# Strassen's scheme for the values of a chunked recurrence, inside a fused HGRN2 + MLA layer

## The chip, the cores and the metric

The kernel is one launch on one core of a Trainium2 chip. The metric is device time of that launch in microseconds (us), the median of a few runs, before against after. A difference under about 0.2% (1.2 us) can't be told from no change here.

## The reference, cut to what matters

One hybrid decoder layer over 512 tokens of 1024 channels. Its first product projects the normalised input onto many column groups; two branches follow, a gated linear recurrence (HGRN2, 8 heads of 128) and multi-head latent attention (MLA), merged by gates:

```
h  = rms_norm(x, g)                              # (512, 1024)
hq, hf, hi, hz, cq, ckv, kr, mz, glog = split(h @ w_in)
v  = hi                                          # the recurrence's values: h @ w_in[:, 2048:3072]
S_t = diag(f_t) S_{t-1} + k_t v_t^T ;  o_t = S_t^T q_t        # chunkwise, per head
y_a = rms_norm(o) * silu(hz) ;  y_b = MLA(cq, ckv, kr) * silu(mz)
m  = sigmoid(g_a) * (y_a @ W_pa) + sigmoid(g_b) * (y_b @ W_pb)
out = rms_norm(x + m @ W_out)
```

The change is about `v`: a 512x1024 by 1024x1024 product. All is float32; each product runs as three matmuls of a high and a low part (hi*hi, hi*lo, lo*hi), so each weight tile is first cast to its high part (ScalarE, line 129) and the rest subtracted (VectorE, line 130).

## The kernel before, in words

**Stages in order of time.** (1) `x` is loaded, normalised, transposed into `hT` (two parts), and the latent columns `c` are projected, in an order written out by hand. (2) The second part of `c` is projected, then `c` is transposed into `cT`. (3) Four head pairs of the recurrence, `hg_pair(0)` to `hg_pair(3)`: each projects F (forget), Q and ZA (gate) with `proj_ch`, and pairs 0 and 2 also project the values of four heads with `proj_tok` (line 606). `hg_forget` makes decays on VectorE and GpSimd, `hg_turned`, `hg_states`, `hg_scores`, `hg_out` and `hg_gate` are small matmuls and elementwise work. (4) Eight MLA heads. (5) The two merge gates, `W_pa`, `W_pb` and `W_out`. The gates, `W_pa` and `W_out` already use a Strassen scheme with seven products (`strassen`, line 943).

**Values before.** `proj_tok` takes 512 columns and runs over four token tiles, eight k-slices and three kinds: 96 matmuls of 512 columns, in pair 0 and again in pair 2. Each reads four weight chunks of 512 KB.

**Order of the work.** Outside blocks marked manual, a planner orders each engine's queue from a simulated timeline; `issue_after` only forbids an earlier place. Each engine works through its own queue in order.

**Weights.** `load_w` takes one of three raw buffers (SP's queue), one of four high and one of four low buffers. After each load it issues one entry of `queued`: copies of weight blocks from HBM to HBM for `BlockSums`, which `step()` later adds to by accumulating transfers on GpSimd's queue (line 803).

**Sums of the activations.** `early_sums(q)` (line 819) makes the four differences of blocks of `hT` that the gates' Strassen products need, half in `hg_pair(0)` behind its forget part, half behind pair 0, and saves them to HBM.

**Memory.** The `cwork` pool (`c_sb`, `ktab` and others) is closed before `mla_a` and `hgrn` are opened; `ya` is a plain tile, first written by `hg_gate`.

Of the kernel before, what the change touches and what calls it, by code (L numbers as in the profile page):

```python
# [18 lines left out]
P = 128  # L19
# [4 lines left out]
H = 8  # L24
# [14 lines left out]
def hybrid_layer(ctx: ExitStack, tc: tile.TileContext, a):  # L39
# [68 lines left out]
    queued = []  # L108

    def load_w(*pieces, to=None):  # L110
# [4 lines left out]
        for src in pieces:  # L115
# [12 lines left out]
            o += n  # L128
        last_hi[0] = nc.scalar.copy(hi[:, :o], raw[:, :o])  # L129
# [51 lines left out]
    kpe = Pair(cpool.tile([P, 2, S], F32R, "kpe")[:])  # L181
    cw = Pool("cwork", "right")
# [23 lines left out]
    x_sb = [st.tile([P, D], F32, "x", bufs=NT) for _ in range(NT)]  # L206
# [49 lines left out]
    def squares(t):  # L256
        sq = st.tile([P, D], F32, "sq", bufs=2)
        nc.scalar.activation(sq[:], x_sb[t][:], AF.Square, accum_out=rss[t][:, 0:1])
        power(rss[t][:, 0:1], rss[t][:, 0:1], 1.0 / D, EPS, neg_half[:, 0:1])
# [17 lines left out]
    def c_product(t, kh, kind, ks=range(4)):  # L277
# [3 lines left out]
        for k in ks:  # L281
            nc.tensor.matmul(ps, hT[l][:, 4 * kh + k, t * P : t * P + P], c_hl[kh][r][:, k * 256 : k * 256 + 256],  # L282
                             start=kh == 0 and kind == 0 and k == 0, stop=kh == 1 and kind == FIN and k == 3)

# [7 lines left out]
    with tc.manual_schedule(engines={mybir.EngineType.PE, mybir.EngineType.Activation, mybir.EngineType.DVE}):  # L292
# [49 lines left out]
        for t in range(1, NT):  # L342
            if t + 2 < NT:
                squares(t + 2)
            for kh in range(2):
                lo[kh]()
# [47 lines left out]
    c_second += [load_c2(j) for j in range(2, 4)]  # L394
    for t in range(NT):
# [4 lines left out]
        nc.scalar.copy(c_sb[:, t, 256:704], ps[:, 0:448])  # L400
    css = cw.tile([P, 2, NT], F32, "css")
# [6 lines left out]
    kd = cw.tile([P, NT, 2, NR], F32, "kd")  # L408
# [17 lines left out]
    ps = ax_tile()  # L426
    for t in range(NT):
        nc.tensor.transpose(ps[:, t * P : t * P + P], kd[:, t].rearrange("p a r -> p (a r)"), ident[:])
    split(*kpe, ps[:])
# [3 lines left out]
    ya = ypool.tile([P, H, S], F32, tag="ya", name="ya")  # L433
    ma_pool = Pool("mla_a", "right")
    qtab = ma_pool.tile([P, 2, S], F32, "qtab")
    nc.gpsimd.dma_start(qtab[:], a["c_qtab"])
# [120 lines left out]
    def hg_out(h, asb, st_, q128, v_sb):  # L557
# [12 lines left out]
        nc.vector.tensor_tensor(on[:].rearrange("p (g v) -> p g v", g=NT), ops[:].rearrange("p (g v) -> p g v", g=NT),  # L570
# [15 lines left out]
    v_sb = [None] * NT  # L586

    def hg_pair(pair, in_forget=None, in_query=None, before_gate=None, last=None):
        cc, hs = pair * 256, (2 * pair, 2 * pair + 1)
        pf = proj_ch(w_in, COL_F + cc, hT)  # L590
# [3 lines left out]
        else:  # L594
            early_sums(kh[0])
# [7 lines left out]
        if pair % 2 == 0:  # L603
            for t in range(NT):
                v_sb[t] = hw.tile([P, 512], F32, f"v{t}")
            proj_tok(w_in, COL_I + cc, hT, lambda t, ps: nc.scalar.copy(v_sb[t][:], ps[:]))
        else:
            zz = gate()
        pq = proj_ch(w_in, COL_Q + cc, hT)
        qq = [hg_query(h, pq[i], kk[i][0], kk[i][2], None if i else in_query) for i, h in enumerate(hs)]  # L610
        step()
# [4 lines left out]
        if pair % 2 == 0:  # L616
# [27 lines left out]
    def mla_turn(pair):  # L644
# [4 lines left out]
        for b in range(4):  # L649
            nc.scalar.dma_start(qs[32 * b : 32 * b + 32, :], qr[32 * (b ^ 1) : 32 * (b ^ 1) + 32, :])  # L650
# [122 lines left out]
    kh = [slice(0, 2), slice(2, 4)]  # L773
    half_t = [slice(0, 256), slice(256, 512)]
    blocks = lambda t: (t[:, 0:4, half_t[0]], t[:, 4:8, half_t[0]], t[:, 0:4, half_t[1]], t[:, 4:8, half_t[1]])
    TERMS = ((0, 0), (1, 1), (0, 1), (1, 0))

    def minus(out, x, y):
        nc.vector.tensor_tensor(out, x, y, op=ALU.subtract)

    def minus_minus(out, x, y):

        nc.vector.scalar_tensor_tensor(out, x, -1.0, y, op0=ALU.mult, op1=ALU.subtract)

    class BlockSums:
# [7 lines left out]
        def start(self):  # L793
            for t, ij in zip(self.t, TERMS):
                for q in kh:
                    queued.append(lambda t=t[:, q], w=self.w[ij][:, q]: nc.sync.dma_start(t, w))

        def add(self, *ns):
            with tc.issue_after(last_pool[0].ins):
                for n in ns:  # L800
                    x = {0: self.w[0, 1], 2: self.w[1, 1], 1: self.t[0], 3: self.t[1]}[n]
                    for q in kh:
                        nc.gpsimd.dma_start(self.t[n][:, q], x[:, q], accum_op=ALU.add)
# [13 lines left out]
    h_dram = [[dram.tile([P, 4, 256], F32, name=f"h{n}{i}") for i in range(2)] for n in range(1, 5)]  # L817
# [496 lines left out]
```

## Time and profile before

| | us |
|---|---|
| median of 3 runs | 607.22 (606.46 to 607.28) |
| the profiled execution, its own time | 606.81 |
| its span, first to last instruction | 605.0 |
| outside the span | 1.8 |

The profile is one execution. PE is TensorE's matmul queue, PEld its weight loads, DVE VectorE, ACT ScalarE, POOL GpSimd, SP the queue that issues most transfers. "Busy" of PE includes the modelled end of each matmul, so two matmuls overlap in it; the distance between starts is what one costs in a stream.

### The profile page before, as it was taken

The page shows a single profiled execution, that of the slowest core. Times are in us where ns is not written, and L with a number is a line of the kernel's source. Part 1 is how long each engine was busy: PE and PEld are TensorE (multiplying, and loading weights), DVE is VectorE, ACT ScalarE, POOL GpSimd, SP SyncE. Part 2 cuts the span into 40 slices and gives each one's busy share as a digit, 9 for nine tenths or more (in the row PEclk, how much of TensorE's full clock was granted, in tenths as well). Part 3 has the DMA queues.
Part 4 walks back from the last instruction along what each step waited for, and adds up shares of the span by engine and source line. Part 5 has one row for each costly group of instructions (what it writes and reads, how often), then busy time and mean ns, then how long its engine had stood idle before and what let it go on. Part 6 is the DMA issues. An engine that isn't in the chain of part 4 may idle for free.

```text
span 605.0 us, 8841 instructions
## 1 busy us (share of the span) xinstructions
PE 595.2 (98%) x3198; PEld 501.4 (83%) x3198; DVE 430.1 (71%) x697; ACT 282.1 (47%) x517; POOL 159.5 (26%) x256
## 2 busy tenths in 40 slices
PE   8999999999999999999999999999999999999994
PEld 5998888888888888888888888888888888888884
DVE  6717988477654648768767686778878878466795
ACT  6555154333314332436555554456656764253553
POOL 3107602384460238524245440300000000000003
PEclk9999999999999999999999999999999999999998
DMA  8449579989889866772369676787666655467313
GB/s 274 157 141 334 171 251 381 261 168 278 209 175 273 174 198 119 186 148 65 68 156 169 153 157 158 203 301 244 190 193 202 196 186 187 134 225 262 105 36 139
DMA packets 73035, 115.34 MB, mean 191 GB/s; under 512 B 7560, under 2 KB 37662, under 8 KB 72992
## 3 DMA queue, kind: packets, MB, share of 16 engines
q1 hardware_dynamic: 63740, 90.99, 46.4%
q0 software_dynamic: 8336, 22.55, 20.8%
q10 hardware_dynamic: 916, 1.25, 0.6%
q8 instruction: 25, 0.41, 0.3%
q14 instruction: 18, 0.15, 0.1%
HBM read 106.38 MB, written 39.85 MB: 242 GB/s over the span
## 4 chain that ended last, share of the span: by engine, by line
PE 89%; DVE 4%; DMA 3%; ACT 2%; issue 1%; POOL 1%; SPq 0%; POOLq 0%; ACTq 0%; DVEq 0%
PE mm_ps L102 19%; PE mm_ps L104 19%; PE mm_ps L103 19%; PE ax_ps L895 16%; PE mm_ps L895 3%; PE ax_ps L760 1%; PE ax_ps L734 1%; DMA x<-x 1%; PE mm_ps L282 1%; PE ax_ps L562 1%; DVE ya L1179 1%; PE ax_ps L564 1%; PE ax_ps L524 1%; PE ax_ps L104 1%; PE ax_ps L103 1%
## 5 line engine op out<-in xcount | busy, mean ns | idle before, releaser
L130 DVE TENSOR_TENSOR w_lo<-w_raw,w_hi 128x1024 fp32r<-128x1024 f32 (+3 forms) x116 | 137.1, 1188 | 72.3 <-ACT w_hi L129 63.7
L129 ACT CAST w_hi<-w_raw 128x1024 fp32r<-128x1024 f32 (+3 forms) x116 | 114.6, 1006 | 124.5 <-PE mm_ps L103 59.4
L102 PE MATMUL mm_ps<-hT,w_hi 128*128 128x512 f32 x256 | 101.4, 396 | 0.0
L103 PE MATMUL mm_ps<-hT,w_hi 128*128 128x512 f32 x256 | 100.1, 391 | 0.0
L104 PE MATMUL mm_ps<-hT,w_lo 128*128 128x512 f32 x256 | 99.7, 392 | 0.0
L102 PE MATMUL mm_ps<-w_hi,hT 128*128 128x512 f32 (+1 forms) x160 | 61.7, 390 | 0.0
L103 PE MATMUL mm_ps<-w_lo,hT 128*128 128x512 f32 (+1 forms) x160 | 61.6, 386 | 0.0
L104 PE MATMUL mm_ps<-w_hi,hT 128*128 128x512 f32 (+1 forms) x160 | 61.4, 385 | 0.0
L102 PEld LDWEIGHTS mm_ps<-hT,w_hi 128*128 128x128 f32 x256 | 48.1, 188 | 9.8 <-DVE z L584 0.3
L104 PEld LDWEIGHTS mm_ps<-hT,w_lo 128*128 128x128 f32 x256 | 48.1, 188 | 9.8
L103 PEld LDWEIGHTS mm_ps<-hT,w_hi 128*128 128x128 f32 x256 | 48.1, 188 | 9.4
L895 PE MATMUL ax_ps<-w_hi,s 128*128 128x512 f32 x208 | 51.5, 390 | 0.0
L895 PEld LDWEIGHTS ax_ps<-w_hi,s 128*128 128x128 f32 x208 | 39.0, 188 | 8.1
L1196 POOL TENSOR_SCALAR ssum<-ssum 128x1 f32<-128x1 f32 x3 | 0.7, 225 | 163.3 <-ACT z L1183 163.2
L104 PEld LDWEIGHTS mm_ps<-w_hi,hT 128*128 128x128 f32 x160 | 30.1, 188 | 5.5
L102 PEld LDWEIGHTS mm_ps<-w_hi,hT 128*128 128x128 f32 x160 | 30.1, 188 | 5.3
L103 PEld LDWEIGHTS mm_ps<-w_lo,hT 128*128 128x128 f32 x160 | 30.1, 188 | 5.2
L742 ACT ACTIVATE p<-ax_ps,sm 128x128 f32<-128x128 f32 (+3 forms) x32 | 16.7, 525 | 35.2 <-DVE sm L741 35.0
L744 POOL TENSOR_SCALAR p<-p,sm 128x128 f32<-128x128 f32 (+3 forms) x28 | 15.6, 560 | 65.4 <-DVE sm L743 52.8
L895 PE MATMUL ax_ps<-w_lo,s 128*128 128x512 f32 x104 | 27.8, 389 | 0.0
L505 POOL TENSOR_TENSOR q<-qi,gh 128x256 f32<-128x256 f32 x8 | 6.9, 866 | 63.0 <-DVE qi L503 63.0
L895 PEld LDWEIGHTS ax_ps<-w_lo,s 128*128 128x128 f32 x104 | 19.5, 188 | 4.1
(323 smaller groups left out, 1210.1 us busy)
## 6 DMA issues: line engine op xcount, KB each, us to landing
w_raw<-w_in SPq DMA_DIRECT2D x54, 512.0 KB, 6.3
g_t<-w_in SPq DMA_DIRECT2D x16, 512.0 KB, 8.2
w_raw<-g_t SPq DMA_DIRECT2D x16, 512.0 KB, 4.9
g_t<-w_in POOLq DMA_DIRECT2D x8, 512.0 KB, 9.7
pa_t<-w_proj_a SPq DMA_DIRECT2D x8, 512.0 KB, 11.4
g_t<-g_t POOLq DMA_DIRECT2D x8, 512.0 KB, 10.4
out_t<-w_out SPq DMA_DIRECT2D x8, 512.0 KB, 6.3
s<-h POOLq DMA_DIRECT2D x8, 512.0 KB, 11.0
```

The lines of the kernel that those rows point to most:

```text
L102: nc.tensor.matmul(ps, lh[lsl], rh[rsl], start=start, stop=False)
L103: nc.tensor.matmul(ps, lh[lsl], rl[rsl], start=False, stop=False)
L104: nc.tensor.matmul(ps, ll[lsl], rh[rsl], start=False, stop=stop)
L129: last_hi[0] = nc.scalar.copy(hi[:, :o], raw[:, :o])
L130: last_lo[0] = nc.vector.tensor_tensor(lo[:, :o], raw[:, :o], hi[:, :o].bitcast(F32), op=ALU.subtract)
L282: nc.tensor.matmul(ps, hT[l][:, 4 * kh + k, t * P : t * P + P], c_hl[kh][r][:, k * 256 : k * 256 + 256], start=kh == 0 and kind == 0 and k ...
L505: last_pool[0] = nc.gpsimd.tensor_tensor(c2_(q64), c4(qi)[:, :, 2:4], bc(gh, 10, 2), op=ALU.mult)
L524: nc.tensor.matmul(sps[:, sl], kt_[:, sl], v_sb[i][:, (h % 4) * P : (h % 4) * P + P], start=True, stop=True)
L562: nc.tensor.matmul(ops[:, sl], asb[:, sl], v_sb[i][:, (h % 4) * P : (h % 4) * P + P], start=True, stop=i == 0)
L742: last_act[0] = nc.scalar.activation(p[:, :n], sps[:, :n], AF.Exp, scale=SCALE, bias=sm[:, 1:2], accum_out=sm[:, 2:3])
L744: scaled_p = (nc.vector if final else nc.gpsimd).tensor_scalar(p[:, :n], p[:, :n], sm[:, 3:4], 0.5, op0=ALU.mult, op1=ALU.mult)
L895: nc.tensor.matmul(ps[:, o : o + n], ap[i][:, k, t * P : t * P + P], w[k // 2][j][:, k % 2, o : o + n], start=fresh and c == 0, stop=c == ...
```

## The change

The values are computed for all eight heads as one 512x1024 by 1024x1024 product in 2x2 blocks by Strassen's scheme: seven block products of 256 tokens, 512 inputs and 512 columns, 24 matmuls of 512 columns each. Five run in pair 0 (`values_first`; the first, `first_u`, ahead of the transposes of `c`), which gives heads 0 to 3 whole and keeps four tiles `v_late`; two run in pair 2 (`values_rest`).

The activation sums are regrouped: S2 and S3 are made ahead of pair 0 (`early_sums`), S1 and S4 behind it (`fetch_rest`). The weight sums live in `ya` (`i_w2`, `i_w3`): one is built by an accumulating transfer on GpSimd's queue, two by VectorE additions, and in pair 1 one is rebuilt by a reload and an accumulating transfer (`RestSum`). `x_sb` now lies in `ya` too. `mla_a` is opened ahead of `cwork`. The transposes of `c` wait for the last matmul of `first_u`'s first tile (`first_mm[0]`). The transposes of `kpe` move behind pair 0's states. The copies for `BlockSums` are queued at the end of `values_first` and not at the start; up to two entries of `queued` leave behind each load through pair 1, then one, then none for a while; `adds` has a new order. The rope swap of pair 0 is issued by GpSimd instead of ScalarE, and `qtab` is loaded behind pair 2.

```
-                if queued:
+                for _ in range(min(len(queued), behind[0])):
...
+    ya = ypool.tile([P, H, S], F32, tag="ya", name="ya")
+    ma_pool = Pool("mla_a", "right")
     cw = Pool("cwork", "right")
...
-    x_sb = [st.tile([P, D], F32, "x", bufs=NT) for _ in range(NT)]
+    x_sb = [ya[:, 2 * t : 2 * t + 2].rearrange("p k c -> p (k c)") for t in range(NT)]
...
+    def early_sums():
...
+        e22, e21, e11 = whole("e22", h22), whole("e21", h21), whole("e11", h11)
+        minus(e22, e22, e21)
+        minus_minus(e22, e22, e11)
+        s2 = keep(2, e22)
+        minus(e21, e11, e21)
+        s3 = keep(3, e21)
...
+    c_lo_last = last_lo[0]
+    for q in kh:
+        nc.sync.dma_start(i_w3[:, q], i_w[0, 1][:, q])
+    for q in kh:
+        nc.gpsimd.dma_start(i_w3[:, q], i_w[1, 1][:, q], accum_op=ALU.add)
+    for q in kh:
+        nc.sync.dma_start(i_w2[:, q], i_w[0, 0][:, q])
...
+    with tc.issue_after(c_lo_last.ins):
+        s_kept = early_sums()
+        for q in kh:
+            nc.vector.tensor_tensor(i_w2[:, q], i_w2[:, q], i_w3[:, q], op=ALU.add)
...
+    def v_product(ap, w, done, banks=None, tile=ax_tile):
+        res = banks or [tile() for _ in range(2)]
+        for t, ps in enumerate(res):
+            for n, (x, k) in enumerate((x, k) for x in range(3) for k in range(4)):
+                i, j = ((0, 0), (1, 0), (0, 1))[x]
+                mm_ = nc.tensor.matmul(ps[:], ap(i, k, t), w[k // 2][j][:, k % 2], start=not banks and n == 0, stop=n == 11,
+                                       skip_group_check=banks is not None)
+            last_mm[0] = mm_
+            done(t, ps)
+        return res
...
+    first_f = proj_ch(w_in, COL_F, hT)
+    first_mm = []
+    first_u = v_product(h11, i_block(0, 0), lambda t, ps: first_mm.append(last_mm[0]))
...
-            nc.tensor.transpose(ps[:, t * P : t * P + P], c_sb[:, t, j * P : j * P + P], ident[:])
+            with tc.issue_after(first_mm[0].ins):
+                nc.tensor.transpose(ps[:, t * P : t * P + P], c_sb[:, t, j * P : j * P + P], ident[:])
...
+        u = first_u
+        for t, ps in enumerate(u):
+            nc.scalar.copy(v_sb[t][:], ps[:])
+        v_product(s2, i_split(i_w2), late(2), u)
+        v_product(s3, i_split(i_w3), late(3), u)
+        w10, raws = [], []
+        for q in kh:
+            w10.append(load_w(i_w[1, 0][:, q]))
+            nc.vector.tensor_tensor(i_w2[:, q], i_w2[:, q], last_raw[0].rearrange("p (k c) -> p k c", k=2), op=ALU.add)
+        v_product(h12, w10, lambda t, ps: nc.vector.tensor_tensor(v_sb[t][:], v_sb[t][:], ps[:], op=ALU.add), tile=mm_tile)
+        v_product(h22, i_split(i_w2), lambda t, ps: nc.scalar.copy(v_sb[2 + t][:], ps[:]), u)
...
+        r = v_product(of_sum(s_late[1]), i_split(i_w2), rest(3), tile=mm_tile)
+        v_product(of_sum(s_late[4]), i_block(1, 1), rest(2), r)
...
-            proj_tok(w_in, COL_I + cc, hT, lambda t, ps: nc.scalar.copy(v_sb[t][:], ps[:]))
-        else:
+            (values_rest if pair else values_first)()
...
-            nc.scalar.dma_start(qs[32 * b : 32 * b + 32, :], qr[32 * (b ^ 1) : 32 * (b ^ 1) + 32, :])
+            (nc.scalar if pair else nc.gpsimd).dma_start(qs[32 * b : 32 * b + 32, :], qr[32 * (b ^ 1) : 32 * (b ^ 1) + 32, :])
```

## Rows read from the trace of the kernel before

**Rows 1.** The page: busy time by engine; PE's busy tenths in 40 slices.

```profile
PE 595.2 (98%) x3198; PEld 501.4 (83%) x3198; DVE 430.1 (71%) x697; ACT 282.1 (47%) x517; POOL 159.5 (26%) x256
...
PE   8999999999999999999999999999999999999994
```

**Rows 2.** The page: the chain that ended last, by engine.

```profile
PE 89%; DVE 4%; DMA 3%; ACT 2%; issue 1%; POOL 1%; SPq 0%; POOLq 0%; ACTq 0%; DVEq 0%
```

**Rows 3.** Stretches: length, busy time (instructions) per engine, clock, DMA share.

```profile
core 0: us, PE busy (x) PEld busy (x) DVE busy (x) ACT busy (x) POOL busy (x), PEclk, DMA share, GB/s
20.00:25.00 5.00, 5.00 (x45) 5.00 (x45) 3.66 (x6) 3.24 (x5) 0.00 (x0) 1.00 0.00 0
...
31.00:37.00 6.00, 6.00 (x32) 5.56 (x31) 0.01 (x1) 1.42 (x5) 0.00 (x0) 1.00 0.92 321
37.00:45.00 8.00, 8.00 (x41) 7.42 (x40) 1.83 (x2) 5.87 (x15) 0.00 (x0) 1.00 0.02 7
45.00:61.00 16.00, 16.00 (x83) 13.57 (x82) 11.82 (x20) 9.12 (x16) 11.70 (x21) 1.00 0.98 324
61.00:83.00 22.00, 22.00 (x104) 18.17 (x103) 21.32 (x32) 7.98 (x13) 9.43 (x14) 1.00 0.50 172
83.00:130.00 47.00, 47.00 (x300) 39.69 (x299) 31.60 (x46) 17.57 (x37) 16.35 (x23) 1.00 1.02 291
130.00:178.00 48.00, 48.00 (x307) 40.70 (x306) 33.30 (x47) 13.08 (x31) 27.73 (x50) 1.00 0.87 218
...
394.00:450.00 56.00, 56.00 (x259) 46.74 (x258) 46.58 (x62) 31.99 (x44) 0.53 (x1) 1.00 0.72 234
```

**Rows 4.** PE's groups by shape: one of the three kinds of `proj_tok` and `W_pb`.

```profile
L102 PE MATMUL mm_ps<-w_hi,hT 128*128 128x512 f32 x128 | 50.2, 395 | 0.0
```

**Rows 5.** The chain in order of time: a run of Strassen matmuls (start, length).

```profile
446.41 32.64 PE ax_ps L895 x144
```

**Rows 6.** PE in order of time: pair 0's first F matmul; the transposes of `c`.

```profile
45.29 0.39 PE L102 MATMUL mm_ps<-hT,w_hi 128*128 128x512 f32 x1
...
54.59 2.34 PE L422 MATMUL ax_ps<-ident,c_sb 128*128 128x128 f32 x20
```

**Rows 7.** VectorE's groups by shape: total, mean ns, idle time before them.

```profile
L130 DVE TENSOR_TENSOR w_lo<-w_raw,w_hi 128x1024 fp32r<-128x1024 f32 x100 | 123.9, 1246 | 64.4 <-ACT w_hi L129 56.3 <-ACT osq L568 6.6 <-PE ax_ps L760 0.9
...
L470 DVE TENSOR_TENSOR_SCAN tf<-f__635,ends 128x512 f32<-128x512 f32 x8 | 10.9, 1358 | 5.5 <-POOL k L468 5.4
...
L471 DVE TENSOR_TENSOR_SCAN pr<-f__635,fr 128x512 f32<-128x512 f32 x8 | 9.8, 1222 | 0.7 <-POOL fr L467 0.2
...
L491 DVE TENSOR_TENSOR k<-ko,gh 128x512 f32<-128x512 f32 x8 | 6.6, 821 | 8.3 <-POOL gh L478 8.3
...
L489 DVE TENSOR_TENSOR ko<-k,tf 128x512 f32<-128x512 f32 x8 | 5.4, 676 | 0.1
...
L466 DVE TENSOR_SCALAR f__635<-tf,c,c 128x512 f32<-128x512 f32 x8 | 4.7, 584 | 2.4 <-ACT tf L465 2.4
...
L424 DVE SCALAR_TENSOR_TENSOR cT<-ax_ps,par,cT 128x512 fp32r<-128x512 f32 x5 | 3.5, 727 | 0.0
```

**Rows 8.** VectorE in order of time: the two ends of its longest early pause.

```profile
30.85 0.16 DVE L390 TENSOR_SCALAR c<-lb 128x8 f32<-128x8 f32 x1
43.17 3.50 DVE L130 TENSOR_TENSOR w_lo<-w_raw,w_hi 128x1024 fp32r<-128x1024 f32 x3 [12.16 <-ACT w_hi L129]
```

**Rows 9.** ScalarE's groups by shape: the weight cast and the values' copy.

```profile
L129 ACT CAST w_hi<-w_raw 128x1024 fp32r<-128x1024 f32 x100 | 103.0, 1050 | 109.0 <-PE mm_ps L103 44.3 <-PE ax_ps L895 24.1 <-issue 10.8
...
L606 ACT COPY v<-mm_ps 128x512 f32<-128x512 f32 x8 | 4.6, 584 | 9.8 <-PE mm_ps L104 9.6
```

**Rows 10.** Transfers: size and median us to landing; an accumulating one is POOLq.

```profile
w_raw<-w_in SPq DMA_DIRECT2D x54, 512.0 KB, 6.3
...
g_t<-w_in POOLq DMA_DIRECT2D x8, 512.0 KB, 9.7
```

**Rows 11.** Tile `g_t`'s copies and accumulating transfers together: us to landing.

```profile
DMA to landing us min/median/max: 3.7/9.1/13.3
```

More of the change, by code (lines that the diff above doesn't have):

```diff
@@ L128, in load_w @@
             o += n
+        last_raw[0] = raw[:, :o]
         last_hi[0] = nc.scalar.copy(hi[:, :o], raw[:, :o])
@@ L344, in hybrid_layer @@
                 squares(t + 2)
-            for kh in range(2):
-                lo[kh]()
+            for n in range(2):
+                lo[n]()
             if t + 1 < NT:
@@ new lines, in hybrid_layer, with add, fetch_rest, whole @@
+    s_late = {}
+    class RestSum:
+        def add(self):
+            with tc.issue_after(last_pool[0].ins):
+                for q in kh:
+                    nc.gpsimd.dma_start(i_w2[:, q], i_w[0, 1][:, q], accum_op=ALU.add)
+    def fetch_rest():
+        items = [lambda q=q: nc.sync.dma_start(i_w2[:, q], i_w[0, 0][:, q]) for q in kh]
+        s_late[1], s_late[4] = kept(1), kept(4)
+        x, y = [ya[:, 2 + i].rearrange("p (k c) -> p k c", k=2) for i in range(2)]
+        for i, q in enumerate(kh):
+            h11, h12, h21, h22 = zip(*[[b[:, q] for b in blocks(t)] for t in hT])
+            def whole(o, hl):
+                nc.vector.tensor_tensor(o, hl[0].bitcast(F32), hl[1].bitcast(F32), op=ALU.add)
+            whole(x, h22), whole(y, h21)
+            minus(x, x, y)
+            split(*s_late[1][i], x)
+            whole(y, h11)
+            minus_minus(x, x, y)
+            whole(y, h12)
+            minus_minus(y, y, x)
+            split(*s_late[4][i], y)
+            for n in (1, 4):
+                items.append(lambda n=n, q=q, hl=s_late[n][i]: save(n, q, hl))
+        queued[0:0] = items
@@ L615, in hg_pair @@
             before_gate()
-        if pair % 2 == 0:
+        if not pair:
+            ps = ax_tile()
+            for t in range(NT):
+                nc.tensor.transpose(ps[:, t * P : t * P + P], kd[:, t].rearrange("p a r -> p (a r)"), ident[:])
+            split(*kpe, ps[:])
             zz = gate()
@@ L770, in mla_out @@
         nc.vector.tensor_tensor(yb[:, h], ops[:], z[:], op=ALU.mult)
[L773 to L783, printed above, removed]
+    copied_parts = set()
     class BlockSums:
@@ L851, in step @@
             if x:
-                x[0].add(x[1])
-    for w in (*gate_w, pa_w, out_w):
-        w.start()
+                x[0].add(*x[1:])
     for pair in range(H // 2 - 1):
+        if pair == 2:
+            behind[0] = 1
         hg_pair(pair)
         if pair == 0:
-            early_sums(kh[1])
+            fetch_rest()
     early = []
+    qtab = ma_pool.tile([P, 2, S], F32, "qtab")
+    nc.gpsimd.dma_start(qtab[:], a["c_qtab"])
     def first_scores():
@@ L984, in hybrid_layer @@
         pools = (ma_pool, mw)
+        behind[0] = min(h, 1)
         if h in (2, 4):
@@ L1014, in hybrid_layer @@
                 turned_q = mla_rotate(*turned_q)
-            step()
+            for _ in range(1 + (h > 4)):
+                step()
         else:
```

127 lines of the change are left out of this document (84 added, 43 removed).

## The prediction

> **What bounds the kernel now.** I read the page's busy line first. PE is busy 98% of the span and its digits are full from the second slice to the last but one [rows 1]; the chain that ended last is 89% PE [rows 2]. So from about 15 us to about 590 us there is hardly a wait to remove, and only fewer or cheaper matmuls, or a new wait, can move the time. Busy time overstates a matmul, because the modelled ends overlap: 395 ns for a 512-column one [rows 4]. What it costs in a stream is the distance between starts, and a run of 144 Strassen matmuls gives 32.64 / 144 = 0.2267 us [rows 5]. Next I read the stretches [rows 3]. PE is full in each. VectorE is the nearest second: 21.32 of 22 us at 61 to 83, yet PE does not wait there, and 46.58 of 56 us (83%) in the gates' Strassen stretch. Transfers are saturated at 83 to 130 (share 1.02), nearly so around it, but idle at 20 to 25 and at 37 to 45. VectorE itself stands still from 31 to 43 [rows 8].
>
> **The matmuls.** Before, values cost 2 x 96 = 192 matmuls of 512 columns; after, 7 x 24 = 168. That is 24 fewer, and 24 x 0.2267 = 5.44 us. Pair 0 gets 24 more (5.44 us longer), pair 2 loses 48 (10.88 us shorter). Transposes and other matmuls stay in number. Since PE does not wait before, 5.44 is also the most that can come out of this; the latency chain at the end is not touched.
>
> **VectorE and ScalarE, in total.** Weight chunks to split rise from 8 to 14: six casts of 1.05 on ScalarE [rows 9], 6.3 us, and six subtractions of 1.25 on VectorE [rows 7], 7.5 us. Activation sums before are 24 VectorE instructions of 128x512; the nearest row is 0.68 us [rows 7], so 16.3 us. After, `early_sums` has six of 128x1024 (priced as a split, 1.25) and four of 0.68, 10.2 us, and `fetch_rest` has 18 of 0.68, 12.2 us: 6.1 us more. Weight sums add four of 1.25, 5.0 us. ScalarE still makes eight copies of a value tile (0.58 each [rows 9]), VectorE gets six more at about 0.68, 4.1 us. VectorE sums to 7.5 + 6.1 + 5.0 + 4.1 = 22.7 us more: 430 becomes 453 of some 600 us, 76%. The gates' stretch runs at 83% with PE full, so in total this is hidden and costs nothing. If the cover were gone, all 22.7 would show, so the places matter.
>
> **Place one, 31 to 45 us.** `early_sums` and two weight additions are 10.2 + 2.5 = 12.7 us, and the pause they fall into is 12.2 us long [rows 8]. Behind them on VectorE stand the splits of pair 0's F weights. PE starts F at 45.29 [rows 6] and reads the low part two matmuls later, at 45.74; the first split ran from 43.17 to about 44.4. The margin is 1.3 us, the work overruns by 0.5, and an instruction in flight can hold 1.25 more. The stall lies between 0 and 0.45; I take 0.2.
>
> The second addition also waits for an accumulating transfer. Early bound: the plain loads use the idle stretch from 20, land by 25 + 6.3 = 31.3 [rows 10], and the accumulating ones 9.7 later, at 41. Late bound: loads leave at 31, land at 37.3, and the accumulating ones take the longest landing seen on `g_t`, 13.3 [rows 11]: 50.6. The early one is likelier, as `x` is consumed by 25 and the queue has nothing else to move then. With T the landing, the F split ends at T + 2.5 + 1.25 and PE stalls T - 42 us: nothing at 41, 8.6 at 50.6.
>
> The landing row for an accumulating 512 KB is 9.7 us in a full queue [rows 10]. The Trainium skill (DMA: Bandwidth & Descriptors, Anatomy of one DMA) fits a GpSimd-issued transfer as 2.0 us plus bytes over 436 GB/s; an estimate from that is 3.2 us. By it T would be about 35 and this stall would not exist even when the loads are late by six; by the row there is no room to spare. I keep the row.
>
> **Place two, 61 to 86 us.** F ends at 45.29 + 48 x 0.2267 = 56.2, the first product at 61.6, and the transposes take 2.3 [rows 6], so S2 runs from 64.0, S3 from 69.4, the fourth from 74.8, the fifth from 80.3 to 85.7. Each product reads its low parts eight matmuls (1.8 us) in: at 71.2, 76.6 and 82.1. `hg_forget` of pair 0 now starts late: `hgrn` lies where `cwork` lay, so its tiles wait for the transposes, and its work falls into this place. VectorE has from about 61.6: five `cT` parts, 3.6; two heads of `hg_forget` at 0.58 + 1.36 + 1.22 + 0.68 + 0.82 = 4.7 [rows 7], 9.3; six splits, 7.5; two additions, 2.5. That is 22.9 us before 82.1, in 20.5 us of time. Pair 0's second forget head (4.7) is not needed until its turned keys, behind Q at about 96; with it put off, 18.2 fits and the stall is nothing. Without, it is about 2.4 us. I take nothing, because before the change VectorE was as full there (97%) and PE did not wait [rows 3].
>
> **Transfers and queues.** Loads for values rise from 8 to 12 of 512 KB, and four accumulating ones come in. Six of the loads and two accumulating ones fall into the early idle stretches or replace loads there. The copies for `BlockSums` that left from 25 us on now start behind `values_first`, at about 85, where the share is already 0.87 to 1.02. SP's queue carries them, and the weight loads stand behind them: a landing of 6.3 becomes perhaps 13.3 at worst [rows 10, 11]. Chunks in `proj_ch` last 24 matmuls, 5.44 us, and three raw buffers make three of them, 16 us, so this is hidden; PE was full under a share of 1.02. GpSimd's queue holds the accumulating transfers ahead of `hg_forget` and `hg_query` work; `RestSum` waits for a reload issued with pair 1's first load, some 20 us earlier. The four rope swaps on GpSimd wait for ScalarE's copy; the rope is read in the MLA stage, a pair later, so even 13.3 us would not show. ScalarE is freed of four issues. `fetch_rest` puts 12.2 us of VectorE work behind pair 0; 83 to 178 holds 31.6 + 33.3 = 64.9 of 95 us now [rows 3], and with 12.2 it would be 77.1, 81%, at the level that the gates bear. I cost all of these at nothing, with up to 2 us above.
>
> **The sum.** Against the profiled execution: 606.81 - 5.44 + 0.2 = 601.6. The median of runs stands 0.41 above that execution, so I predict 602.0.
>
> **Rival one: VectorE becomes the bound in place two, no change.** If the planner puts both forget heads ahead of S3's splits, those end at 61.6 + 3.6 + 9.3 + 2.5 = 77.0 against 71.2: 5.8 us late, the gain is gone, and the median is 607.22 - 5.44 + 5.8 = 607.6. For it: VectorE's 97% at 61 to 83. Against it: the planner sees these waits, and half of that order costs only 2.4 (604.2).
>
> **Rival two: slower, by the accumulating transfer in front of F's splits.** Place and price are those of T above. It decides from a stall of 5.44 + 1.2 = 6.6, so T past 48.6; at 50.6 the median is 607.22 - 5.44 + 8.6 = 610.4. For it: 9.7 to 13.3 us of landing, and one late load suffices. Against it: two idle stretches of the transfers ahead of it, and this place is early enough for the planner to put F's splits ahead of the additions.
>
> The Trainium skill (TensorE: Matmul & The Clock Gate, Architectural detail) says that VectorE's and ScalarE's queues are strictly first in, first out, and this speaks against the change: nothing ready passes a waiting addition. No row of this trace tests it by itself. By that rule rival two costs the whole T - 42; were ready work let past, it would cost nothing.
>
> **Rival three: part of the gain.** Late weight loads behind the copies, or a forget head in the way: 1 to 4 us of stalls, 603 to 606.
>
> **How the numbers follow.** Forecast, 600.9 to 602.8: 0.55. Rival three, 602.8 to 606.0: 0.22. Rival one and its like, 606.0 to 608.4: 0.08. Rival two or any stall sum above 6.6: 0.15. So faster 0.77, same 0.08, slower 0.15, with 0.2% (1.2 us) about what a measurement can tell. The low end is the full 5.44 off the median, 601.8, less the runs' own spread (0.8); the high end, 606.5, leaves out the slower case and the top of rival one. The range is 600.9 to 606.5; the likeliest case's own is 600.9 to 602.8.
>
> **What would show it.** PE's count falls by about 24, to about 3174, and its digits stay full. Pair 0's stage is some 5 us longer, pair 2's some 11 shorter. VectorE's total rises by about 23 us, ScalarE's by 6. Right on place one: no PE idle before F, and the additions end by 44. Right on place two: no PE idle between 56 and 86, and the second forget head behind the last splits. Wrong: PE idle released by a low part, by an accumulating transfer or by a landing weight load, or a stage after pair 0 that is longer than before.

## The result and the profile after

The change makes the kernel slower: 623.52 us (619.81 to 625.80, four runs) against 606.84 beside it, ratio 1.0271 with a 95% interval of 1.0219 to 1.0322. The profiled execution took 623.64, its span 621.9.

The page of the changed kernel: busy time, PE's busy tenths in 40 slices, the granted clock.

```profile
PE 598.3 (96%) x3174; PEld 501.8 (81%) x3174; DVE 453.2 (73%) x717; ACT 286.8 (46%) x523; POOL 168.2 (27%) x264
...
PE   8999799999999699989999999999999999999995
...
PEclk9999799999999799989999999999999999999999
```

Against [rows 1], PE has 24 fewer matmuls, VectorE 23.1 us more, ScalarE 4.7 more. The work is what was forecast. New are three holes in PE's digits, in the slices at 62, 202 and 264 us, and a dip of the clock with each.

Stretches of the changed kernel: the first two against [rows 3], the third against the line of the kernel before beneath, the last two cut finer (same columns).

```profile
45.00:61.00 16.00, 16.00 (x73) 13.04 (x72) 12.97 (x17) 5.65 (x10) 10.96 (x17) 1.00 0.60 197
61.00:83.00 22.00, 18.73 (x81) 14.95 (x80) 19.11 (x25) 10.72 (x18) 11.17 (x24) 0.84 0.07 15
...
178.00:226.00 48.00, 41.92 (x206) 34.39 (x206) 29.18 (x40) 12.16 (x17) 16.21 (x26) 0.93 0.85 220
...
67.00:70.00 3.00, 3.00 (x7) 2.40 (x8) 3.00 (x5) 0.35 (x1) 0.94 (x2) 0.50 0.03 5
...
208.00:212.00 4.00, 4.00 (x10) 3.04 (x10) 1.77 (x2) 0.41 (x1) 0.00 (x0) 0.50 0.90 291
```

The kernel before, 178 to 226:

```profile
178.00:226.00 48.00, 48.00 (x303) 40.43 (x302) 23.58 (x32) 17.52 (x35) 7.29 (x10) 1.00 0.85 215
```

At 61 to 83 PE is busy 18.73 of 22 us at a mean clock of 0.84; at 178 to 226 it is 41.92 of 48. Transfers are nearly idle in the first (0.07), and at 0.85 in the second.

PE's waits in the changed kernel: us in total, times, longest.

```profile
PE mm_ps L102 <- DVE z L676: 6.4, 2, 6.1
PE ax_ps L616 <- ACT kt L608: 2.8, 1, 2.8
PE ax_ps L478 <- ACT v L694: 1.7, 1, 1.7
PE ax_ps L522 <- DVE cT L524: 1.5, 1, 1.5
PE ax_ps L251 <- DVE zero L347: 1.2, 1, 1.2
PE ax_ps L670 <- DVE k L662: 1.0, 1, 1.0
```

Of these only the wait for `zero` was there before. New waits sum to about 14 us (6.4 + 2.8 + 1.7 + 1.5 + 1.0 and some small ones). The mean granted clock is 0.984 against 0.996, and 0.012 x 621.9 is another 7.5. Together some 22; the span grew by 16.9, and with the 5.4 that the matmuls gave back that is 22.3. The balance is rough, since some of the lower clock lies in idle time.

**Stall one, 61 to 73 us.** PE, then VectorE, in order of time.

```profile
60.87 1.47 PE L522 MATMUL ax_ps<-ident,c_sb 128*128 128x128 f32 x12
63.87 1.31 PE L522 MATMUL ax_ps<-ident,c_sb 128*128 128x128 f32 x8 [1.53 <-DVE cT L524]
66.92 1.22 PE L478 MATMUL ax_ps<-w_hi,qn 128*128 128x512 f32 x2 [1.74 <-ACT v L694]
67.94 1.05 PE L478 MATMUL ax_ps<-w_hi,kn 128*128 128x512 f32 x2
```

```profile
59.44 1.23 DVE L700 TENSOR_TENSOR ya<-ya,w_raw 128x1024 f32<-128x1024 f32 x1
60.79 2.36 DVE L174 TENSOR_TENSOR w_lo<-ya,w_hi 128x1024 fp32r<-128x1024 f32 x2
63.07 1.40 DVE L524 SCALAR_TENSOR_TENSOR cT<-ax_ps,par,cT 128x512 fp32r<-128x512 f32 x2
```

Before, the twenty transposes ran in one go [rows 6], though VectorE came to read the first of them only 4.7 us after their start (kernel before, VectorE):

```profile
59.27 0.74 DVE L424 SCALAR_TENSOR_TENSOR cT<-ax_ps,par,cT 128x512 fp32r<-128x512 f32 x1
```

Now they stop after twelve, three `ax` banks: the first product holds two more banks and waits for ScalarE's copy, and the three do not come free until VectorE, behind an addition and two splits of later products' weights, begins its readings at 63.07. Then the second product waits for ScalarE, which copies the first product out behind `cT`'s last parts. When it starts, at 66.92, two matmuls are 0.85 to 1.02 us apart (0.50 of the clock at 67 to 70) where 0.453 is the price at 1.00 [rows 5]; the pace is back at 72.9. From 66.92 to 73.36, sixteen matmuls took 6.44 us and not 3.63: 2.8 us of clock behind 3.3 us of waits.

**Stall two, 201 to 213 us.** SP and GpSimd's issues, ScalarE, PE, in order of time.

```profile
187.13 3.29 SPq L122 DMA_DIRECT2D w_raw<-w_uq  x3
...
191.29 10.59 SPq L957 DMA_DIRECT2D pa_t<-w_proj_a  x1
```

```profile
180.89 2.44 POOL L966 DMA_DIRECT2D g_t<-w_in  x2
189.72 1.72 POOL L966 DMA_DIRECT2D g_t<-g_t  x2
191.37 1.59 POOL L999 DMA_DIRECT2D qtab<-c_qtab  x1
```

```profile
205.79 0.51 ACT L131 CAST w_hi<-w_raw 128x384 fp32r<-128x384 f32 x1 [10.36 <-DMA w_raw<-w_uq]
206.20 0.59 ACT L675 ACTIVATE z<-mm_ps 128x512 f32<-128x512 f32 x1
```

```profile
207.57 0.80 PE L102 MATMUL mm_ps<-hT,w_hi 128*128 128x512 f32 x1 [6.08 <-DVE z L676]
```

PE waits for a bank of ZA; the bank waits for `z` on ScalarE; and `z` stands behind a cast that has waited 10.36 us for three 64 KB pieces of `w_uq`. Around these loads lie four accumulating transfers (`g_t` on GpSimd's queue), `qtab` and a copy that SP took 10.59 us to issue. The kernel before, GpSimd's last additions ahead of the same loads, then SP's issue of the loads:

```profile
174.78 1.70 POOL L803 DMA_DIRECT2D g_t<-g_t  x2
```

```profile
184.76 1.40 SPq L121 DMA_DIRECT2D w_raw<-w_uq  x3
```

The same loads before and after, in the transfers issued at 183 to 212 (KB, median us to landing); first before, then after:

```profile
w_raw<-w_uq SPq DMA_DIRECT2D x3, 64.0 KB, 5.2
```

```profile
g_t<-g_t POOLq DMA_DIRECT2D x2, 512.0 KB, 12.2
...
qtab<-c_qtab POOLq DMA_DIRECT2D x1, 512.0 KB, 13.6
w_raw<-w_uq SPq DMA_DIRECT2D x3, 64.0 KB, 17.1
```

The share of the transfers over the stage is the same, 0.85 before and after. What differs is what is issued close to the small loads: before, two additions 10 us ahead of them and the next only at 202.56; after, two additions 4 to 6 us ahead, and two more and the table within 5 us behind the first of them.

**Stall three, 267 to 273 us.** It has the same form; ScalarE, then PE:

```profile
268.23 0.72 ACT L131 CAST w_hi<-w_raw 128x640 fp32r<-128x640 f32 x1 [3.65 <-DMA w_raw<-w_ukv]
...
269.35 0.85 ACT L608 COPY kt<-ax_ps 128x384 f32<-128x384 f32 x2
```

```profile
269.88 2.23 PE L616 MATMUL ax_ps<-v,kt 128*128 128x128 f32 x12 [2.83 <-ACT kt L608]
```

### The profile page after: what moved, and what is told of

It is laid out like the page before. It is cut to its first block, busy times and chain, and to the rows that moved or that the text cites. A ratio compares the mean times of both kernels' runs of the same rounds, so it can differ in the third digit from the quotient of the medians.

```text
span 621.9 us, 8824 instructions
## 1 busy us (share of the span) xinstructions
PE 598.3 (96%) x3174; PEld 501.8 (81%) x3174; DVE 453.2 (73%) x717; ACT 286.8 (46%) x523; POOL 168.2 (27%) x264
## 4 chain that ended last, share of the span: by engine, by line
PE 43%; DVE 4%; ACT 2%; DMA 1%; issue 1%; POOL 1%; POOLq 0%; ACTq 0%; DVEq 0%
PE ax_ps L1033 14%; PE mm_ps L102 7%; PE mm_ps L104 7%; PE mm_ps L103 7%; PE mm_ps L1033 3%; PE ax_ps L928 1%; PE ax_ps L902 1%; DMA w_raw<-w_in 1%; DVE ya L1319 1%; DVE w_lo L132 1%; ACT w_hi L131 1%; PE ax_ps L104 1%; PE ax_ps L103 1%; DMA w_raw<-w_out 1%; PE ax_ps L102 1%
## 5 line engine op out<-in xcount | busy, mean ns | idle before, releaser
L131 ACT CAST w_hi<-w_raw 128x1024 fp32r<-128x1024 f32 (+3 forms) x114 | 112.8, 1006 | 141.6 <-PE mm_ps L103 48.3
L102 PE MATMUL mm_ps<-w_hi,hT 128*128 128x512 f32 (+1 forms) x96 | 36.9, 388 | 0.0
L104 PE MATMUL mm_ps<-w_hi,hT 128*128 128x512 f32 (+1 forms) x96 | 36.5, 382 | 0.0
L103 PE MATMUL mm_ps<-w_lo,hT 128*128 128x512 f32 (+1 forms) x96 | 36.5, 382 | 0.0
L912 POOL TENSOR_SCALAR p<-p,sm 128x128 f32<-128x128 f32 (+3 forms) x28 | 15.2, 549 | 52.1 <-DVE sm L911 41.8
L597 POOL TENSOR_TENSOR q<-qi,gh 128x256 f32<-128x256 f32 x8 | 8.5, 1057 | 76.5 <-DVE qi L595 76.5
L102 PE MATMUL mm_ps<-cT,w_hi 128*128 128x512 f32 x52 | 20.6, 397 | 0.0
L104 PEld LDWEIGHTS mm_ps<-w_hi,hT 128*128 128x128 f32 x96 | 18.0, 188 | 3.0
L104 PE MATMUL mm_ps<-cT,w_lo 128*128 128x512 f32 x52 | 20.4, 392 | 0.0
## 6 DMA issues: line engine op xcount, KB each, us to landing
s<-h POOLq DMA_DIRECT2D x8, 512.0 KB, 20.5
```

The costliest lines, as they stand in the source:

```text
L102: nc.tensor.matmul(ps, lh[lsl], rh[rsl], start=start, stop=False)
L103: nc.tensor.matmul(ps, lh[lsl], rl[rsl], start=False, stop=False)
L104: nc.tensor.matmul(ps, ll[lsl], rh[rsl], start=False, stop=stop)
L597: last_pool[0] = nc.gpsimd.tensor_tensor(c2_(q64), c4(qi)[:, :, 2:4], bc(gh, 10, 2), op=ALU.mult)
L912: scaled_p = (nc.vector if final else nc.gpsimd).tensor_scalar(p[:, :n], p[:, :n], sm[:, 3:4], 0.5, op0=ALU.mult, op1=ALU.mult)
```

## The experiments

The first theory: stall one is the order of the work on the `ax` banks and VectorE (A); stalls two and three are loads held up by other transfers. Rivals are named with each run. The changed kernel itself spreads over 6 us, so for single runs the waits are read rather than a few microseconds.

Part of that spread is the clock, which falls behind a wait in one execution and stays up behind the same wait in another. Run 5 leaves stall one as it is, and there the clock did not fall; PE at the second wait, and the stretch that stood at 0.50 in the changed kernel:

```profile
67.20 0.72 PE L478 MATMUL ax_ps<-w_hi,qn 128*128 128x512 f32 x2 [1.74 <-ACT v L694]
```

```profile
67.00:70.00 3.00, 2.80 (x12) 2.33 (x13) 3.00 (x6) 0.64 (x2) 1.23 (x2) 1.00 0.02 5
```

The first wait is 1.53 us there as well. Run 3 is like run 5 in this; in runs 2 and 4 the clock fell as in the changed kernel, and in run 13 for a shorter time. So some 3 us of a single run's time can be chance. The wait for `z` has a spread too: 4.4, 4.6, 3.5 and 4.4 us in runs 1, 2, 6 and 13, which leave stall two's additions, copies and table as they are, against 6.1.

**1. Transposes first.** The first product goes behind `c`'s transposes.

```
-    first_u = v_product(h11, i_block(0, 0), ...)     # ahead of the transposes
...
         nc.vector.scalar_tensor_tensor(cT[1][:, j], ps[:], ...)
+    first_u = v_product(h11, i_block(0, 0), ...)
```

> The transposes of c and their evacuation go ahead of the first value product, as in the kernel before; all else is the change. Theory A (the stall at 61 to 73 us is a chain of waits in order: the first product holds two of five banks, so the second group of transposes waits for a bank, ScalarE's value copies stand behind its evacuations, and the second product waits for those copies): the 3.3 us of PE idle there and the half clock behind it go, the time falls by 6 to 9 us, to about 615 to 617. Rival B (VectorE has too much work there whatever the order): the idle time moves to the second or third product's low parts and the time stays within 2 us of 623.

Measured 616.72 us. The transposes run in one go, and the clock stays at 1.00, which by itself shows nothing. One wait of 2.1 us is left in place of 1.5 and 1.7, PE then VectorE:

```profile
60.28 2.11 PE L478 MATMUL ax_ps<-w_hi,hT 128*128 128x512 f32 x8 [2.13 <-DVE cT L522]
```

```profile
58.34 1.22 DVE L174 TENSOR_TENSOR w_lo<-ya,w_hi 128x1024 fp32r<-128x1024 f32 x1
59.48 1.40 DVE L522 SCALAR_TENSOR_TENSOR cT<-ax_ps,par,cT 128x512 fp32r<-128x512 f32 x2
```

The order is a part of stall one, a third of its waits; what is left stands behind a split of a later product's weights (58.34). The other two stalls stay (4.4 and 2.7 us).

**2. The sums behind pair 0 later**, a rival for stall one: `fetch_rest` stood among the readings of `c`.

```
         if pair == 0:
-            fetch_rest()
+            with tc.issue_after(last_on[0].ins):
+                fetch_rest()
```

> The activation sums S1 and S4 (12 us of VectorE work) may not be placed ahead of pair 0's normalised output; all else is the change. Theory A: VectorE had only some 2 us of these sums in front of the cT evacuations, so the stall at 61 to 73 shrinks by 1 to 2 us at most, and the time stays above 620. Rival B (VectorE's volume makes the stall): the stall goes, 614 to 617. Either way the waits at 201 and 267 us should stay unless the saves of these sums, now later, change the transfers.

Measured 628.23, with both waits of stall one unchanged (1.5 and 1.7) and a new one of 3.3 us at 165. That rival falls.

**3. The rope's table later**, behind pair 0's exchange.

```
-    nc.gpsimd.dma_start(qtab[:], a["c_qtab"])
...
+    with tc.issue_after(last_swap[0].ins):
+        nc.gpsimd.dma_start(qtab[:], a["c_qtab"])
```

> The rope table's 512 KB load is issued behind pair 0's rope swap (some 30 us later) and not at 191 us; all else is the change. Theory C (a crowd of transfers in GpSimd's queue, with this table in it, holds up the rope weights that ScalarE waits 10.4 us for at 195 to 206): with a fifth of that crowd gone the rope weights land 2 to 4 us sooner, the 6.1 us of PE idle at 201 falls to 2 to 4, time 618 to 621. Rival D (the table is nothing, the crowd is the copies and the accumulating transfers): no change at 201.

Measured 619.48; the wait at 205 us is 3.1 in place of 6.1, both as forecast by theory C. Yet it does not show that the table has a share: the loads of `w_uq` landed in 14.5 us, and in 14.8 to 16.0 in runs 1, 2, 6 and 13, which have the table in its place; 3.1 us is close below their 3.5 to 4.6. Some 3 us of the time are the clock at stall one.

**4. No additions into the copies.** This leaves out the accumulating transfers of `BlockSums`.

```
-            if x:
-                x[0].add(*x[1:])
+            if x and len(x) == 1:
+                x[0].add()
```

> Leaves out the 16 pairs of accumulating transfers that build the weight sums of the gates, W_pa and W_out (the one for the values stays), so those products use unfinished sums. It tells how much of the two later stalls is theirs. Theory C and rival D: without them the transfers' queues are free at 180 to 275, the PE idle at 201 (6.1 us) and at 267 (2.8 us) goes with the half clock behind it, 9 to 13 us in all, time 610 to 614; the stall at 61 to 73 stays. Rival E (the loads are late because SP's queue issues them late, behind copies): the two stalls stay, above 620.

Measured 608.93, a little below the 610 to 614 expected. Of the longer waits, only those of stall one are left:

```profile
PE ax_ps L478 <- ACT v L694: 1.7, 1, 1.7
PE ax_ps L522 <- DVE cT L524: 1.5, 1, 1.5
```

So stalls two and three need the accumulating transfers; here the loads of `w_uq` landed in 2.5 us. But the kernel before had as many and no wait.

**5. Two steps of additions moved.** The steps behind the forget gates of pairs 2 and 3 issue the transfers at 190 and 256 us. They are left out there and caught up in MLA (an empty place in `adds` goes too).

```
-        if pair:
+        if pair == 1:
             step()
...
-            for _ in range(1 + (h > 4)):
+            for _ in range(1 + (h > 2)):
```

> Edit: the changed kernel, with the addition steps behind the forget gates of pairs 2 and 3 left out and caught up in MLA's heads 3 to 5. The run without any addition into the copies (608.93 us) showed that these accumulating transfers make the stalls at 200 and 267 us. Theory A: it is those two steps' transfers, issued within 15 us ahead of the stalls beside the loads of w_uq and w_ukv. Then the wait of 6.4 us at 206 and that of 2.8 us at 269, and the half clock behind them, go; the stall at 61 to 73 us stays: 612 to 615 us. Rival B: it is the sum of all accumulating transfers and copies on the rings, not these two. Then both waits stay at over half their length and the time is 619 us or more.

Measured 613.74: the waits for `kt` and of 6.1 us for `z` are gone (0.8 is left, later), the loads of `w_uq` landed in 8.8 us, and the waits of stall one stay. It is these two steps. Of the 9.8 us below the changed kernel some 3 are the clock at stall one. Two new waits came, 1.5 us for `k` at 279 and 1.3 us for `kn` at 357.

**6. Transposes first, and VectorE's additions behind them** (`last_ct` is the last reading of a transposed bank).

```
+            with tc.issue_after(last_ct.ins):
                 nc.vector.tensor_tensor(i_w2[:, q], i_w2[:, q], last_raw[0]..., op=ALU.add)
```

> Edit: the first product of the values is put behind c's transposes (as in the run of 616.72 us, which kept 2.1 us of wait at 60 us), and now VectorE's two additions of w10 to the raw buffer also come behind the last reading of a transposed bank. Theory A: the 2.1 us were VectorE's in-order queue, where those additions and the early splits stood ahead of c's readings. Then no wait over 0.5 us is left between 56 and 75 us, and the time is 614 to 616 us. Rival B: the 2.1 us are the pace of the readings themselves (1.4 us on VectorE for a bank of transposes of some 1.2 us on TensorE). Then a wait of 1.5 us or more stays there and the time is 616 to 618 us.

Measured 613.59; the wait at 60 us falls from 2.1 to 1.1. That is between the two theories, under 0.5 and over 1.5: the additions were half of it.

**7. Runs 5 and 6 together.**

> Edit: both of the above at once (first product behind c's transposes with the additions behind them; no addition step behind the forget gates of pairs 2 and 3). Theory A: the three stalls are separate and their prices add. Then of the 16.7 us that the changed kernel lost, some 8 us come back at 61 to 73 us and some 9 to 11 at 200 and 267 us: 603 to 607 us, at or below the kernel before. Rival B: a stall that is taken away comes back in a later stage (the loads run sooner into the copies). Then 609 to 614 us.

Measured 610.76, where theory A had 603 to 607. Singly they gave 9.8 and 9.9 us, together 12.8; even with the 3 us of chance in run 5 taken off, the prices do not add, and the rival holds. The two waits that run 5 brought are longer, 2.3 us at 274 and 1.8 us at 352; for the second, ScalarE, then PE:

```profile
349.93 1.05 ACT L131 CAST w_hi<-w_raw 128x1024 fp32r<-128x1024 f32 x1 [3.94 <-DMA w_raw<-w_in]
350.88 0.58 ACT L173 CAST kn<-mm_ps 128x512 fp32r<-128x512 f32 x1
```

```profile
352.89 0.59 PE L102 MATMUL mm_ps<-w_hi,cT 128*128 128x512 f32 x1 [1.78 <-DVE kn L174]
```

The additions moved to 320 to 333 us, and the load behind them is late there in the same way.

**8. Run 7 with the table late.**

> Edit: as the kernel before this one in the list, and the table of the rope (512 KB on GpSimd's queue) is loaded behind the exchange of pair 0 instead of at its place beside the loads of w_uq. Alone this took the wait at 205 us from 6.1 to 3.1 us (619.48 us). Theory A: with the addition steps gone the queue has room, and the table's place is worth under 1 us: 602.5 to 606.5 us, faster than the kernel before by 0.1 to 0.7%. Rival B: the table is a cause of its own, so this is 3 us or more below the kernel beside it. Rival C: the table comes late for MLA's second rotation and TensorE waits there: slower than the kernel beside it.

Measured 611.63 (609.25 to 612.88), ratio 1.0070 (1.0047 to 1.0093), no better than run 7 and above the 602.5 to 606.5 of theory A. Neither rival shows; with the additions gone, the table's place is worth nothing that these runs can show.

**9. Copies early**, as before the change: queued ahead of pair 0's F.

```
+    for w in (*gate_w, pa_w, out_w):
+        w.start()
+    behind[0] = 1
     first_f = proj_ch(w_in, COL_F, hT)
```

> Edit: the changed kernel, with the 32 copies of weight blocks into the sums' buffers queued ahead of pair 0's F (as in the kernel before, where they ran from 25 to 212 us) in place of behind pair 0's values (83 to 330 us): one behind each load up to the values, three behind each of w10's two, then two as now. Theory A: the accumulating transfers did not stall the kernel before, at the same number, since the copies were out of their way by 212 us; so with early copies the waits of 6.4 us at 206 and 2.8 us at 269 go or fall under 1 us each, and 61 to 73 us stays as it is or is up to 2 us worse: 612 to 616 us. Rival B: the place of the copies does not matter, the additions stall the loads beside them by themselves: both waits stay at over half, 619 us or more. Rival C: early copies delay the loads of the early sums and of the first product: a new wait of over 3 us between 35 and 60 us.

Measured 618.53. The wait for `kt` is gone, that for `z` is 3.3, and stall one grew (3.7 and 1.7). Between the theories: the copies' place is a cause of stall three, whose wait is 2.5 to 2.8 us in all runs that leave its copies and additions alone (1, 2, 3, 6 and 13). Of stall two it is not shown to be one: `w_uq` landed in 15.2 us, and 3.3 is close below the 3.5 to 4.6 of the runs without this edit.

**10. Run 6 with copies early.**

> Edit: copies early as in the kernel beside it, and the first product behind c's transposes with VectorE's additions behind them (alone 613.59 us). Theory A: both causes are taken away and what is left is the matmuls saved and small waits: 602 to 606 us, at or below the kernel before. Rival B: as with the addition steps moved (610.76 us), a stall comes back in another stage: 608 us or more.

Measured 613.49 (608.42 to 616.49), ratio 1.0096 (1.0066 to 1.0126). The wait for `z` at 199 us stays at 3.1, and that for `kt` is gone again. Theory A had 602 to 606; the runs spread over 8 us.

**11. Run 6 without the additions** (leaves them out).

> Edit: first product behind c's transposes with the additions behind them, and no accumulating transfer into the copied blocks (leaves those additions out; the copies stay). It bounds what can be won: no stall of theory A is left. If the 24 matmuls saved are worth their 5.4 us, this is 600 to 603 us. Rival: if some of the loss lies elsewhere (TensorE's pace in the new products, VectorE's 23 us), it stays above 605 us.

Measured 602.81, 4.1 under the kernel before, no wait over 1.2 us. This is the whole of the forecast gain of 5.4 but 1.3 us, in a single run. It also shows the small loads by themselves, over the whole run:

```profile
w_raw<-w_uq SPq DMA_DIRECT2D x12, 64.0 KB, 2.5
```

**12. All the transfers' edits at once:** run 7, copies early, table late; then variants that also give pair 0 back the step it had behind its query (as before), with one (the second) or both (the third) of the steps of run 5 left out.

> Edit: first product behind c's transposes with the additions behind them, copies early, no addition step behind the forget gates of pairs 2 and 3 (caught up from MLA's head 3 on), the rope's table behind pair 0's exchange. Theory A (it is how much lies on the rings at one place): no wait over 1.5 us at 190 to 275 us, and with the copies ended before MLA the doubled additions at 320 to 350 us do not stall either: 602 to 605.5 us. Rival B (the doubled steps stall in MLA by themselves): a wait of 1.5 us or more at 320 to 360 us stays, 606 to 610 us.

> Edit: first product behind c's transposes with the additions behind them, copies early, the table behind pair 0's exchange, the addition step behind pair 0's query back (as before; the early copies allow it) and only pair 2's step behind its forget gate left out. Theory A: 602 to 606 us, no wait over 1.5 us at 190 to 210 us. Rival: the step behind pair 3's forget gate (issued some 10 us ahead of 265 us) stalls kt's reading there, as in the changed kernel (2.8 us): 606 to 609 us.

> Edit: as the kernel beside it with pair 0's step back, but with both steps behind the forget gates of pairs 2 and 3 left out. Theory A: 602 to 605.5 us; against the kernel without pair 0's step, the doubled steps in MLA end one head sooner. Rival: as there, a wait of 1.5 us or more in MLA: 606 us or more.

Measured 607.96, 607.70 and 607.79. In the first and the third, a wait for `kn` in MLA stays (1.7 us, the rival, and 1.3, just under the 1.5 that the rival asks). In the second, no wait over 1 us is left behind 70 us, and its rival falls. All three missed their forecasts, 605.5 to 606 at most; all three have the wait left at 55 to 63 us, which run 14 prices at some 1.2 (607.70 to 606.53). There, in the second, VectorE, then PE:

```profile
58.26 2.34 DVE L174 TENSOR_TENSOR w_lo<-ya,w_hi 128x1024 fp32r<-128x1024 f32 x2
60.53 3.37 DVE L564 SCALAR_TENSOR_TENSOR cT<-ax_ps,par,cT 128x512 fp32r<-128x512 f32 x5
```

```profile
61.32 3.09 PE L478 MATMUL ax_ps<-w_hi,hT 128*128 128x512 f32 x8 [2.16 <-DVE cT L564]
```

**13. The exchange of rows back on ScalarE's queue**, the changed kernel otherwise.

```
-            (nc.scalar if pair else nc.gpsimd).dma_start(qs...)
+            nc.scalar.dma_start(qs...)
```

> Edit: the changed kernel with pair 0's exchange of rows for the rope issued on ScalarE's queue again, as in the kernel before. Theory A: that part of the change has no share in the loss: 621 to 626 us. Rival: GpSimd's queue, where the exchange stands behind the additions, is what makes the stall at 267 us: then 3 us or more below.

Measured 622.04, inside the changed kernel's own spread, with all three stalls. That part has no visible share.

**14. The second product's splits behind the transposes too**, on the second kernel of 12.

```
-        v_product(s2, i_split(i_w2), late(2), u)
+        with tc.issue_after(last_ct.ins):
+            w_s2 = i_split(i_w2)
+        v_product(s2, w_s2, late(2), u)
```

> Edit: the kernel with pair 0's step back (607.70 us), and VectorE's two splits of the second product's weights (2.34 us, ahead of its five readings of c's transposes at 58.3 us) put behind the last of these readings. Theory A: the wait of 2.2 us at 61 us goes, and the clock stays up behind it: 604 to 606 us, at or just below the kernel before. Rival B: the second product then waits for its splits instead: no gain, 607 to 609 us.

Measured 606.53 (605.76 to 607.04), ratio 0.9994 (0.9985 to 1.0004). Theory A had 604 to 606; the wait at 61 us that it names is gone, and PE does not wait for the splits instead:

```profile
57.32 3.37 DVE L564 SCALAR_TENSOR_TENSOR cT<-ax_ps,par,cT 128x512 fp32r<-128x512 f32 x5
60.61 2.50 DVE L174 TENSOR_TENSOR w_lo<-ya,w_hi 128x1024 fp32r<-128x1024 f32 x2
```

**15. Run 14 with the copies begun only behind w10's loads.**

```
-    behind[0] = 1
+    behind[0] = 0
...
-        behind[0] = 3
+        behind[0] = 4
```

> Edit: as the kernel beside it, and the copies begin only behind w10's loads (at some 60 us, four behind each), so that none runs beside the loads for the early sums and the first product. Theory A (the early copies beside those loads cost as well): 602 to 604.5 us, faster than the kernel before by 0.4 to 0.8%, and 1 us or more below the kernel beside it. Rival: the copies are hidden there, and later ones collide again: same as the kernel beside it or slower, with a wait at 190 to 210 us.

Measured 609.36, ratio 1.0043 (1.0028 to 1.0059). The rival: the same copies, run later, collide again, though at 257 us and not at 190 to 210; the wait for `kt` is back at 3.2 us behind this cast:

```profile
255.94 0.72 ACT L131 CAST w_hi<-w_raw 128x640 fp32r<-128x640 f32 x1 [3.93 <-DMA w_raw<-w_ukv]
```

So the copies' place matters by itself (2.8 us between runs 14 and 15), as does the place of two steps of additions.

## Why the prediction was wrong

**The matmuls: right.** PE's count is the forecast 3174, and with all stalls out the gain appears (run 11; part of it in PE's busy time in run 14, 591.6 against 595.2).

**VectorE and ScalarE in total: the sums right.** VectorE rose by 23.1 us (22.7 forecast), ScalarE by 4.7 (6.3). That they cost nothing holds within 1.3 us in run 11, which has the same work; in run 14 a wait of 1.2 us for `pr` at 112 stands behind a split on VectorE (110.30 to 111.90), so there some of it shows.

**Place one: right in its cost, and narrowly.** The second addition and the F splits, on VectorE:

```profile
42.90 1.23 DVE L465 TENSOR_TENSOR ya<-ya 128x1024 f32<-128x1024 f32 x1 [0.65 <-DMA ya<-w_in]
44.05 2.35 DVE L132 TENSOR_TENSOR w_lo<-w_raw,w_hi 128x1024 fp32r<-128x1024 f32 x2
```

T was 42.9, between the early and the late bound, and the additions ended at 44.1; PE had no idle time there. By the prediction's T - 42 this is a stall of 0.9 us. None came because the formula puts both additions behind T, and here the first had run at 39.82. The first split ended at about 45.2, and PE read the first low part at 45.35, in F's fifth matmul (44.44 is the first); the prediction's reading, two matmuls in, is wrong for the kernel before too (46.20, not 45.74). These accumulating transfers took 12.0 us (median of two). The estimate of 3.2 us from the Trainium skill (DMA: Bandwidth & Descriptors, Anatomy of one DMA) is a quarter of that; the trace decides, and by it the margin held only because the loads left early, at 23.57 to 25.7.

**Place two failed: "I take nothing".** Its reason, that VectorE had been as full before and PE did not wait, compared busy shares and left out the banks. With two of them held by the first product, twelve transposes fit instead of twenty, and readings that had been free to come late set the pace; splits and additions for later products stood ahead of them. Undoing the order took a third of the waits away (3.3 to 2.1, run 1), moving the additions behind the readings half of the rest (1.1, run 6), and moving the splits too all of it (run 14). The prediction counted 22.9 us of VectorE work in 20.5 and asked whether it fitted, not what stood ahead of the readings of the transposes. Rival one had this place, but as forget heads in the way, and at 5.8 us. It is 6.1 us in the profiled execution, 3.3 of waits and 2.8 of lower clock, with no forget head ahead of the readings; runs 4 and 11, both without the additions into the copies, also lie 6.1 apart. That rival one's price is so near is luck.

**"Transfers and queues" failed: "I cost all of these at nothing, with up to 2 us above".** Two steps of it. "A landing of 6.3 becomes perhaps 13.3 at worst": it became 17.1, for pieces of 64 KB. And "three raw buffers make ... 16 us, so this is hidden" looked at the wrong reader: PE did not need these chunks yet, but ScalarE's cast of them stood ahead of `z` and `kt`, which PE did need. The Trainium skill (TensorE: Matmul & The Clock Gate, Architectural detail) calls such queues strictly first in, first out; the trace agrees, `z` starts 0.4 us after the cast that waited 10.36. The prediction weighed that rule for VectorE in place one and not for ScalarE here. Rival three had late weight loads, behind the copies and at 1 to 4 us; it is right for stall three, where both copies and additions are needed, and short of the additions for stall two. Run 4 puts both later stalls with their clock at some 14 (623.52 to 608.93). Rival two had the sign, as 0.15 of the chances, and the same agent, accumulating transfers, in another place.

What makes the loads late is settled in part. Accumulating transfers are needed (run 4), and the place of two steps of them takes both later stalls away (run 5). For stall three the copies' place does so too (runs 9 and 10; runs 14 and 15). That the table or the copies have a share in stall two is not shown. The parts do not add up, since additions moved to MLA stall loads there (run 7). How the transfers hold each other up these runs do not show.

**Not in the sum at all:** PE's pace behind a stall. The clock was at 0.50 for 5 to 6 us behind each of the first two stalls, and on average 0.61 at 270 to 273 behind the third; about a third of the loss by the mean clock (7.5 of 22 us). That it fell behind stall one was in part chance: with the same two waits it stayed at 1.00 in runs 3 and 5.

**What stays open.** Run 14 has the matmul gain and no stall of the three, and is still not faster. PE is busy 3.6 us less, not 5.4, and idle 3.0 us more in its shorter span: small waits for `pr` and `k` (2.2 and 1.0 us) that the kernel before did not have. From F's first matmul to the long Strassen run of [rows 5] it takes 400.40 us (44.74 to 445.14) against 401.12 (45.29 to 446.41), so 0.7 of the 5.4 us arrives there; those waits and some 0.2 beside them are 3.4 of the rest, and 1.3 is not assigned. From there to the end it takes 0.7 us longer than before, for a reason that stays open. No version that computes the same beats the kernel before; 602.81 leaves the additions out.

## What to carry to other kernels

Before moving a product, list the PSUM banks that it holds until it is copied out, and who reads the remaining ones: a late reader is free only while the banks last. For each late load, look at what stands behind its cast in that engine's queue and not only at when TensorE needs the chunk. Keep bulk accumulating transfers away from small loads in time, by their issue times and not by the stage's mean share, and read a stall of a few microseconds in several executions, since the slower clock behind it may come or not.

## What was not expected of the hardware

- The granted clock fell to 0.50, its lower level of 1.2 GHz, behind 6.08 us of idle time and behind two shorter waits (1.53 and 1.74 us, with transposes between), and stayed there until about 212.5 and 72.9 us. Whether it falls is not settled by the length of the wait: behind the same two waits it stayed at 1.00 in runs 3 and 5; behind a single wait of 2.16 us it fell in run 10 and the second kernel of 12 and did not in the first and third of 12; behind 3.53 us in run 6 and 3.16 us in run 15 it did not fall.
- SP took 10.59 us to issue one 512 KB copy (0.56 is usual in the kernel before); the next load on its queue left at 201.99.
- Three 64 KB loads landed in 17.1 us close to four accumulating transfers and a 512 KB table, in 8.8 with two of the four moved away (run 5), in 5.2 before, and in 2.5 without the additions (run 4).
